# A residual block with linear attention: the DeltaNet keys turned to token order in 32x32 blocks by VectorE and the DRAM store

## The chip, the core and the metric

The kernel runs on one core of one Trainium2 chip. The core has TensorE (PE, matmuls and transposes against an identity), VectorE (DVE), ScalarE (ACT), GpSimd (POOL), and SyncE (SP), whose queue issues most of the DMAs; ACT and POOL issue some as well. The engines run their own instruction lists in order and wait for each other by semaphores. The metric is the device time of one execution in microseconds (us). Before the change it is 1882.36 us, the median of 3 runs (1882.15 to 1883.33).

## The reference

A hybrid residual block of width 1024 on 1024 tokens in float32: one wide projection feeds a gated linear attention branch (GLA, 4 heads) and a gated DeltaNet branch (GDN, 8 heads of 128); their gated sum is projected, and a squared-ReLU MLP follows. The change touches the GDN keys only:

```python
d_qkv = jax.nn.silu(causal_short_conv(d_qkv, gdn_conv_w))
d_q, d_k, d_v = jnp.split(d_qkv, [GDN_QK, 2 * GDN_QK], axis=-1)
d_k = l2_norm(d_k.reshape(bsz, s, GDN_HEADS, GDN_DK))
...
a_mat = jnp.where(strict, jnp.einsum('bhnid,bhnjd->bhnij', kb, k) * decay_mat, 0.0)
...
state = dc[..., None, None] * state + jnp.einsum('bhcd,bhcv->bhdv', ks, v_new)
```

Each key needs its l2 norm over the 128 channels of its head, for every token, and the state update needs the keys with tokens on the partitions.

## The kernel before

The wide projection is done as dense blocks: a block multiplies 128 columns of `w_in` (split in a high and a low part, `wH` and `wL`) with the normalised input (`hH`, `hL`) into one of two PSUM tiles `pm`, in 8 steps over the contraction. Each step is three rows of two 128x512 matmuls, in the order `hH,wH`, `hL,wH`, `hH,wL`, and one step is a tick of the program's clock. Everything else is hung on ticks: `at(dt, fn)` puts `fn` into an agenda, and it is emitted between two ticks. Until the second block of the branch gates every engine and SP keep the order in which the program emits; after that, the tile scheduler may reorder. The printed order of an engine's instructions is fixed when the kernel is built.

The first two key heads are made in the opening stage; six more dense blocks (`dense_n(6)`) give heads 2 to 7, then eight blocks give the branch gates (`branch_gate`). A finished key block is copied out by ACT (`key_copy`), gets three convolution taps and a SiLU on DVE (tile `cv`, channels on partitions, tokens along the free dimension), and then `key_head` works on it:

- `kT_d[h]` is stored as it is.
- `transposes(hf)`: four 128x128 TensorE transposes per half head into a PSUM tile of the `pa` pool (4 buffers).
- `squares(hf)`: ACT squares the four PSUM pieces with `accum_out`, which leaves the sums of squares per token in `ssK`, and copies the half into `ktok`; a store then writes `kt_d[h]`, tokens on rows. It is read again in the GDN heads, from 545 us on.
- `decays`, `grams`, `times`, `spill`: exponentials of the gate decays on ACT (tile `gr`), the products of keys with keys on TensorE, their product on DVE (`a`), and stores to `X_d`, `a21_d` and `Dt_d`.

`key_norms` adds EPS to `ssK`, takes the inverse root on DVE, transposes two results on TensorE (`nbrC`, `beC`) and stores them. From them `solve` starts: it loads `X_d`, runs 30 steps of elimination on DVE on two tiles (`X_1848` and `X_1849` in the order before, `X_1766` and `X_1767` after), and stores and reloads results; the ACT queue issues the stores `U_d`, `A_d` and `B_d`. Meanwhile the branch gates and then the first GLA head are computed. Their weights come by SP (`raw`), and ACT makes `wH` and DVE `wL`. `gla_gate(0)` lies in the same stretch: two products `lrS,wlrS`, then ACT, POOL and a scan on DVE (tiles `zm`, `b`).

`quad` is a constant 128x128 matrix with ones where row and column agree modulo 32; a matmul with it sums the four groups of 32 partitions.

Of the kernel before, what the change touches and what calls it, by code (L numbers as in the profile page):

```python
# [12 lines left out]
AF = mybir.ActivationFunctionType  # L13
ALU = mybir.AluOpType
# [36 lines left out]
def block_kernel(ctx: ExitStack, tc: tile.TileContext, x, c, ada_w, ada_b, pre_mix_w, post_mix_w,  # L51
# [25 lines left out]
    def t4(shape=(128, 1024), dt=F32, p="t", tag="w4"):  # L77
        return w4.tile(list(shape), dt, tag=tag, name=nm(p), bufs=tag_bufs[tag])
# [4 lines left out]
    def pat(shape=(128, 512)):  # L83
        return pa.tile(list(shape), F32, tag="pa", name=nm("pa"))
# [407 lines left out]
    def first_tiles():  # L492
        pk, pl = [pmt(), pmt()], [pat(), pat()]
        warm(pk[0][:, 0:128], 4)

        def wk_low(i):
            V.tensor_tensor(wk[i][1], raw_k[:, :, i * 128:(i + 1) * 128], wk[i][0].bitcast(F32), ALU.subtract)

        def mm(w, d, wlo, hlo, start, stop):

            for hf in range(2):
                hs_ = slice(hf * 512, (hf + 1) * 512)
                if w == 2:
                    last["pe"] = T.matmul(pl[hf][:64, :], wS[:, d, :], h_rhs(d, hf, hlo), start=start, stop=stop).ins
                else:
                    last["pe"] = T.matmul(pk[w][:, hs_], wk[w][wlo][:, d, :], h_rhs(d, hf, hlo), start=start, stop=stop).ins

        def a_(p, ws=(0, 2, 1)):
            for d in (2 * p, 2 * p + 1):
                for w in ws:  # L510
                    mm(w, d, 0, 0, d == 0, False)

        def b_(p, w):
            for d in (2 * p, 2 * p + 1):
                mm(w, d, 1, 0, False, False)

        def c_(p, w):
            for d in (2 * p, 2 * p + 1):
                mm(w, d, 0, 1, False, d == 7)

        wk_low(0)
        low(0)
        wk_low(1)
        a_(0, (0,))
        b_(0, 0)
        a_(0, (1,))

        fill = {1: ((c_, 0, 0), (b_, 0, 1), (c_, 0, 1)),
                2: ((a_, 0, (2,)), (a_, 1, (2,)), (b_, 1, 0), (c_, 1, 0)),
                3: ((c_, 0, 2), (c_, 1, 2), (b_, 2, 0), (b_, 1, 1), (c_, 1, 1))}  # L530
        for p in range(1, 4):
            f = [lambda e=e: e[0](*e[1:]) for e in fill[p]]
            ada_pe(p)
            ada_out(p)
            f[0]()
            ada_fin(p)
            ada_cols(p)
            high(p)
            if p == 1:
                A.copy(wS[:, :, 0:32], raw_lba)  # L540
            for fn in f[1:]:
                fn()
            low(p)
            if p == 1:
                V.tensor_tensor(wS[:, :, 32:64], raw_lba, wS[:, :, 0:32].bitcast(F32), ALU.subtract)
            if p == 2:
                ahead[1] = next(ahead[0])
            a_(p, (0, 1) if p == 1 else (0, 2, 1))
        b_(3, 0)
        c_(2, 0)  # L550
        c_(3, 0)
        y0 = key_copy(0, pk[0])
        c_(2, 2)
        c_(3, 2)
        sb, sb2 = t4((64, 1024), p="lba"), t4((64, 1024), p="lb2")
        for hf in range(2):
            A.copy(sb2[:, hf * 512:(hf + 1) * 512], pl[hf][0:64, :])
        for p in (2, 3):
            b_(p, 1)
        for p in (2, 3):  # L560
            c_(p, 1)
        for s_ in (1, 2, 3):
            key_tap(0, pk[0], y0, s_)
        t0 = key_tanh(y0)
        y1 = key_copy(1, pk[1])
        V.tensor_copy(sb[0:32], sb2[32:64])
        V.tensor_add(sb[0:32], sb[0:32], sb2[0:32])
        key_silu(y0, t0)
        for s_ in (1, 2, 3):
            key_tap(1, pk[1], y1, s_)  # L570
        return sb, y0, y1
# [177 lines left out]
    def key_head(h, k, on, tr, sq, ex, gram, times_):  # L749

        z = {}

        def transposes(hf):
            z[hf] = pt = pat()
            for i in range(4):
                T.transpose(pt[:, i * 128:(i + 1) * 128], k[:, (hf * 4 + i) * 128:(hf * 4 + i + 1) * 128], ident)

        def squares(hf):
            if not hf:
                z["tok"] = t4(p="ktok")  # L760
            pt = z.pop(hf)
            for i in range(4):
                j = hf * 4 + i
                A.activation(z["tok"][:, j * 128:(j + 1) * 128], pt[:, i * 128:(i + 1) * 128], AF.Square,
                             accum_out=ssK[:, h * 8 + j:h * 8 + j + 1])
            A.copy(z["tok"][:, hf * 512:(hf + 1) * 512], pt)

        def decays(hf):

            gr = Dk[h]  # L770
            for t in range(hf * 4, hf * 4 + 4):
                A.activation(gr[:, t * 128:(t + 1) * 128], gr[:, t * 128:(t + 1) * 128], AF.Exp,
                             bias=gcN[:, h * 8 + t:h * 8 + t + 1])

        def grams(hf):
            z["g", hf] = pt = pat()
            for i in range(4):
                kk = k[:, (hf * 4 + i) * 128:(hf * 4 + i + 1) * 128]
                T.matmul(pt[:, i * 128:(i + 1) * 128], kk, kk, start=True, stop=True)

        def times(hf):
            if not hf:
                z["a0"] = t4(p="a0")
            h_ = slice(hf * 512, (hf + 1) * 512)
            V.tensor_mul(z["a0"][:, h_], z.pop(("g", hf)), Dk[h][:, h_])

        def spill():
            Dk.pop(h)
            a3 = r3(z["a0"])
            xv = X_d[h * 16:(h + 1) * 16].rearrange("(t e) j i -> e j t i", e=2)  # L790
            DMA.dma_start(xv[0], a3[0:64, :, 0:64])
            DMA.dma_start(xv[1], a3[64:128, :, 64:128])
            DMA.dma_start(a21_d[h], a3[0:64, :, 64:128])

        on(tr[0], lambda: DMA.dma_start(kT_d[h], k))
        for hf in range(2):
            on(tr[hf], lambda hf=hf: transposes(hf))
            on(sq[hf], lambda hf=hf: squares(hf))
            on(ex[hf], lambda hf=hf: decays(hf))
            on(gram[hf], lambda hf=hf: grams(hf))  # L800
            on(times_[hf], lambda hf=hf: times(hf))
        on(sq[1] + 1, lambda: DMA.dma_start(kt_d[h], z["tok"]))
        on(ex[1] + 1, lambda: DMA.dma_start(Dt_d[h], Dk[h]))
        on(times_[1] + 1, spill)
        if h > 3:
            on(ex[0] - 8, lambda: load_decay(h))
            on(ex[0] - 3, lambda: mask_decay(h))
# [1 line left out]


    def key_norms():
        V.tensor_scalar(ssK, ssK, EPS, None, ALU.add)
        r = rsqrt(ssK, 64)
        V.tensor_mul(rbC, r, betaC)
        V.scalar_tensor_tensor(nbrC, rbC, -1.0, r, ALU.mult, ALU.mult)
        V.scalar_tensor_tensor(beC, beC, -1.0, r, ALU.mult, ALU.mult)

        n2 = nbrC.rearrange("p (t e) -> p e t", e=2)
        V.tensor_copy(nbrX[64:128], n2[64:128, 0])
        V.tensor_copy(nbrX[0:64], n2[64:128, 1])  # L820
        ps = pat()
        T.transpose(ps[0:64, 0:128], nbrC, ident)
        T.transpose(ps[0:64, 128:256], beC, ident)
        nb = t4((128, 256), p="nbr")
        V.tensor_copy(nb[0:64], ps[0:64, 0:256])
        ST.dma_start(be_d.rearrange("h (t q) -> (h t) q", q=128), nb[0:64, 0:128])
        ST.dma_start(ner_d.rearrange("h (t q) -> (h t) q", q=128), nb[0:64, 128:256])
# [623 lines left out]
    def masks():  # L1451
# [3 lines left out]
                        pattern=[[1, 128]], channel_multiplier=-1)  # L1455
        G.tensor_copy(cmask, causal)

    sb_lba, *keys = first_tiles()
    masks()
    raws0[C_DK + 512] = load_w(w_in, C_DK + 512)  # L1460
# [3 lines left out]
    def on(t, fn):  # L1464
        at(begin + t - clock[0], fn)
# [477 lines left out]
    def turn(hf, a, g):  # L1943

        pt = pat()
        for i in range(2):
            for e in range(2):
                T.transpose(pt[:, i * 256 + e * 128:i * 256 + e * 128 + 128],
                            xhs[4 * hf + a + e][:, (2 * g + i) * 128:(2 * g + i + 1) * 128], ident)
        if F[hf][g] is None:  # L1950
            F[hf][g] = pair_tile("F")
        for i in range(2):
            k = 2 * g + i
            o, src = F[hf][g][:, i, a * 128:(a + 2) * 128], pt[:, i * 256:(i + 1) * 256]
            if hf == 0 and (g % 2 if a else g > 1):
                V.tensor_scalar(o, src, am2[:, k:k + 1], sh2[:, k:k + 1], ALU.mult, ALU.add)
            else:
                A.activation(o, src, AF.Identity, scale=am2[:, k:k + 1], bias=sh2[:, k:k + 1])
# [579 lines left out]
```

## Time and profile before

| what | value |
|---|---|
| median of 3 runs | 1882.36 us |
| profiled execution: its time, its span | 1881.92 us, 1880.2 us |
| DVE, ACT, POOL busy share of the span | 74%, 47%, 8% |
| queue q1, share of 16 DMA engines | 45.4% |
| first and last `ktok` square on ACT | 75.6 us, 178.2 us |
| first load of `kt_d` in a GDN head | 545.6 us |

The profile describes one execution. A row of the timeline is: start in us, duration in us, engine, line, operation, output<-inputs, shape, and how many instructions were merged; in brackets the idle time of the engine just before and what ended it. All lines read L38, a helper, so groups are told apart by tiles. Matmuls are pipelined, so the duration of one is longer than the distance between the starts of two. A number after an underscore in the printed orders is a buffer, and buffer numbers differ between the two kernels.

### The profile page before, as it was taken

What the parts mean: (1) busy time and instruction counts of PE and PEld (TensorE: products, weight loads), DVE (VectorE), ACT (ScalarE), POOL (GpSimd) and SP (SyncE); (2) the same over time, 40 slices, a digit from 0 to 9 for tenths busy, and PEclk for the clock granted to TensorE, in tenths of its full rate; (3) what the DMA queues carried; (4) which work ended last, traced back from release to release, by engine and by line L of the source; (5) the groups of instructions that cost most, each with busy time, mean ns of one, the idle gap of its engine ahead of it and who ended that gap; (6) DMA issues with size and microseconds to landing.
All of it is one profiled execution on the core that took longest, in us unless ns stands there. A gap on an engine that the chain in (4) does not pass through costs nothing. (4 is left out here: it accounts for less than half of the span.)

```text
span 1880.2 us, 26321 instructions
## 1 busy us (share of the span) xinstructions
PE 1855.1 (99%) x10119; PEld 1556.2 (83%) x10119; DVE 1393.6 (74%) x2166; ACT 883.7 (47%) x1529; POOL 156.0 (8%) x148
## 2 busy tenths in 40 slices
PE   7999999999999999999999999999999999999998
PEld 5788888989898888888888888878888888888886
DVE  5664744968766677778788678986787877778887
ACT  5574324242333444444664555668644446443333
POOL 2120111010110000000101001000022210000001
PEclk9999999999999999999999999999999999999999
DMA  9695563223125454544868657256667668163425
GB/s 313 208 266 181 168 146 102 79 79 113 57 80 158 126 145 145 144 145 145 262 176 223 217 141 203 84 174 208 217 208 250 215 228 317 58 224 111 158 101 101
DMA packets 253341, 313.79 MB, mean 167 GB/s; under 512 B 72770, under 2 KB 178704, under 8 KB 253216
## 3 DMA queue, kind: packets, MB, share of 16 engines
q1 hardware_dynamic: 222608, 274.73, 45.4%
q0 software_dynamic: 14336, 22.44, 6.6%
q10 hardware_dynamic: 16272, 14.95, 2.5%
q8 instruction: 79, 1.29, 0.3%
q14 instruction: 46, 0.38, 0.1%
HBM read 231.67 MB, written 80.41 MB: 166 GB/s over the span
## 5 line engine op out<-in xcount | busy, mean ns | idle before, releaser
L38 PE MATMUL pm<-hH,wH 128*128 128x512 f32 x864 | 285.9, 412 | 0.0
L38 PE MATMUL pm<-hL,wH 128*128 128x512 f32 x864 | 269.0, 393 | 0.0
L38 PE MATMUL pm<-hH,wL 128*128 128x512 f32 x864 | 267.1, 390 | 0.0
L38 PE MATMUL pm<-oH,wB 128*128 128x512 f32 x672 | 214.5, 394 | 0.0
L38 PE MATMUL pa<-w,yH 128*128 128x512 f32 (+1 forms) x696 | 212.4, 387 | 0.0
L38 PEld LDWEIGHTS pm<-hH,wL 128*128 128x128 f32 x864 | 162.2, 188 | 36.8
L38 PEld LDWEIGHTS pm<-hL,wH 128*128 128x128 f32 x864 | 162.1, 188 | 35.9
L38 PEld LDWEIGHTS pm<-hH,wH 128*128 128x128 f32 x864 | 145.1, 190 | 17.0
L38 DVE TENSOR_TENSOR w<-raw,w 128x512 fp32r<-128x512 f32 (+1 forms) x144 | 125.6, 875 | 40.9 <-ACT w L38 37.4
L38 PEld LDWEIGHTS pa<-w,yH 128*128 128x128 f32 x696 | 130.1, 188 | 27.0 <-DVE ya L38 0.4
L38 PEld LDWEIGHTS pm<-oH,wB 128*128 128x128 f32 x672 | 126.2, 188 | 25.7 <-DMA wB<-in_w_branch_gla_dram 0.2
L38 ACT CAST w<-raw 128x512 fp32r<-128x512 f32 (+1 forms) x144 | 99.5, 711 | 89.0 <-DVE raw L38 79.8
L38 PE MATMUL pa<-w,yL 128*128 128x512 f32 (+1 forms) x348 | 134.5, 387 | 0.0
L38 PE MATMUL pm<-oL,wB 128*128 128x512 f32 x336 | 130.8, 389 | 0.0
L38 PE MATMUL pa<-oB,w 128*128 128x512 f32 x480 | 111.9, 391 | 0.8 <-DVE oB L38 0.5
L38 PEld LDWEIGHTS pa<-oB,w 128*128 128x128 f32 x480 | 89.6, 188 | 20.2 <-DVE oB L38 1.3
L38 ACT CAST wH<-raw 128x1024 fp32r<-128x1024 f32 x62 | 64.5, 1047 | 83.0 <-PE pm L38 51.1
L38 DVE SCALAR_TENSOR_TENSOR cv<-pm,ccol,cv 128x1023 f32<-128x1023 f32 (+2 forms) x72 | 92.0, 1278 | 14.1 <-ACT cv L38 12.9
L38 DVE TENSOR_TENSOR wL<-raw,wH 128x1024 fp32r<-128x1024 f32 x62 | 75.9, 1227 | 33.1 <-ACT wH L38 33.0
L38 PE MATMUL pm<-oT,w 128*128 128x512 f32 x384 | 90.8, 389 | 0.0
L38 PE MATMUL pa<-oT,w 128*128 128x512 f32 x384 | 90.8, 389 | 0.0
L38 DVE TENSOR_TENSOR ya<-pa,ya 128x512 f32<-128x512 f32 (+1 forms) x83 | 55.9, 682 | 43.7 <-PE pa L38 43.7
(423 smaller groups left out, 3725.8 us busy)
## 6 DMA issues: line engine op xcount, KB each, us to landing
yL<-y_d SPq DMA_DIRECT2D x53, 512.0 KB, 7.2
raw<-in_mlp_w_dram SPq DMA_DIRECT2D x23, 1024.0 KB, 6.1
raw<-in_w_in_dram SPq DMA_DIRECT2D x18, 1024.0 KB, 7.3
raw<-in_w_in_dram SPq DMA_DIRECT2D x32, 512.0 KB, 4.7
araw<-in_ada_w_dram SPq DMA_DIRECT2D x32, 512.0 KB, 3.8
raw<-in_mlp_w_dram SPq DMA_DIRECT2D x18, 512.0 KB, 5.3
araw<-in_ada_w_dram SPq DMA_DIRECT2D x32, 256.0 KB, 6.9
sl<-sg_d SPq DMA_DIRECT2D x16, 512.0 KB, 7.2
```

Of the source, the lines that this page charges most:

```text
L38: r = fn(*args, **kw)
```

## The change

The TensorE transposes go. DVE transposes each half of `cv` in 32x32 blocks into one tile (still called `ktok`); four DMAs per head, each from 32 partitions, put the blocks in their places in `kt_d[h]`. ACT squares the turned tile in one instruction into a new tile `kj`, and DVE sums groups of 32 into 32 columns of a new tile `ssr`, which lives through the whole stage. `key_norms` first multiplies `quad` with `ssr`, which adds the four channel groups, and four small DVE instructions put the sums in `ssK`.

```diff
-        def transposes(hf):
-            z[hf] = pt = pat()
-            for i in range(4):
-                T.transpose(pt[:, i * 128:(i + 1) * 128], k[:, (hf * 4 + i) * 128:(hf * 4 + i + 1) * 128], ident)
-
-        def squares(hf):
+        def turn(hf):
             if not hf:
-                z["tok"] = t4(p="ktok")
-            pt = z.pop(hf)
-            for i in range(4):
-                j = hf * 4 + i
-                A.activation(z["tok"][:, j * 128:(j + 1) * 128], pt[:, i * 128:(i + 1) * 128], AF.Square,
-                             accum_out=ssK[:, h * 8 + j:h * 8 + j + 1])
-            A.copy(z["tok"][:, hf * 512:(hf + 1) * 512], pt)
+                z["kb"] = t4(p="ktok")
+            h_ = slice(hf * 512, (hf + 1) * 512)
+            V.transpose(z["kb"][:, h_], k[:, h_])
+
+        def spread():
+
+            dst = kt_d[h].rearrange("(b i) (t c j) -> c i t b j", i=32, t=8, j=32)
+            for c_ in range(4):
+                DMA.dma_start(dst[c_], z["kb"][32 * c_:32 * c_ + 32].rearrange("i (t b j) -> i t b j", t=8, j=32))
+
+        def squares():
+            z["kj"] = t4(p="kj")
+            A.activation(z["kj"], z["kb"], AF.Square)
+
+        def sums(hf):
+            o = h * 32 + hf * 16
+            V.reduce_sum(ssr[0][:, o:o + 16], r3(z["kj"][:, hf * 512:(hf + 1) * 512], 16), axis=mybir.AxisListType.X)
...
-            on(tr[hf], lambda hf=hf: transposes(hf))
-            on(sq[hf], lambda hf=hf: squares(hf))
+            on(tr[hf], lambda hf=hf: turn(hf))
+            on(sq[1] + 1 + hf, lambda hf=hf: sums(hf))
...
-        on(sq[1] + 1, lambda: DMA.dma_start(kt_d[h], z["tok"]))
+        on(sq[1], squares)
+        on(tr[1] + 1, spread)
...
     def key_norms():
-        V.tensor_scalar(ssK, ssK, EPS, None, ALU.add)
+        ps = pat()
+        T.matmul(ps[:, 0:256], quad.rearrange("p a b -> p (a b)"), ssr[0], start=True, stop=True)
+        for c_ in range(4):
+            q = slice(32 * c_, 32 * c_ + 32)
+            V.tensor_scalar(ssK[q], ps[q, 0:256].rearrange("p (x c) -> p c x", c=4)[:, c_], EPS, None, ALU.add)
...
+    ssr = [t4((128, 256), p="ssr")]
```

On SP, around the store of head 6's keys, the rows before are:

```order
L38 DMA kT_d_446<-cv_1387 128x1024
L38 DMA Dt_d_462<-gr_1431 128x1024
L38 DMA kt_d_454<-ktok_1534 128x1024
L38 DMA X_d<-a_1589 64x8x64 x2
L38 DMA a_d_470<-a_1589 512x1x64
L38 DMA raw_1624<-in_w_in_dram 128x8x256
```

and now:

```order
L38 DMA kT_d_446<-cv_1333 128x1024
L38 DMA kt_d_454<-ktok_1457 256x4x32 x4
L38 DMA Dt_d_462<-gr_1368 128x1024
L38 DMA X_d<-a_1511 64x8x64 x2
L38 DMA a_d_470<-a_1511 512x1x64
L38 DMA raw_1548<-in_w_in_dram 128x8x256
```

One store of whole rows has become four, ahead of `Dt_d`; the load of the gates' weights (`raw`) is still the sixth name in the list.

On DVE, from the gates' small chain (`s`) of the first key block, the rows before are:

```order
L38 TENSOR_SCALAR s_776<-s_776,dtb 64x128
L38 SCALAR_TENSOR_TENSOR cv_760<-si_795,cv_760 128x1024
L38 TENSOR_SCALAR s_776<-s_776 64x128
L38 TENSOR_TENSOR wL_833<-raw_182,wH_787 128x1024
L38 TENSOR_SCALAR s_776<-s_776 64x128 x2
L38 TENSOR_TENSOR s_776<-s_776 64x128
L38 RECIPROCAL s_776<-s_776 64x128
L38 TENSOR_TENSOR s_776<-s_776 64x128 x2
L38 SCALAR_TENSOR_TENSOR s_776<-s_776 64x128
```

and now:

```order
L38 STREAM_TRANSPOSE ktok_799<-cv_726 128x512
L38 TENSOR_SCALAR s_777<-s_777,dtb 64x128
L38 SCALAR_TENSOR_TENSOR cv_761<-si_796,cv_761 128x1024
L38 TENSOR_SCALAR s_777<-s_777 64x128
L38 STREAM_TRANSPOSE ktok_799<-cv_726 128x512
L38 TENSOR_TENSOR wL_821<-raw_182,wH_788 128x1024
L38 TENSOR_SCALAR s_777<-s_777 64x128 x2
L38 TENSOR_TENSOR s_777<-s_777 64x128
L38 RECIPROCAL s_777<-s_777 64x128
L38 TENSOR_TENSOR s_777<-s_777 64x128
L38 TENSOR_REDUCE ssr_504<-kj_832 128x16
L38 STREAM_TRANSPOSE ktok_851<-cv_761 128x512
```

A second reduction follows these, and then the rest of the chain; three transposes and two reductions now stand ahead of its end.

Also on DVE, inside the elimination, the first rows of the GLA gate (`zm` from `pa`) stand before between these:

```order
L38 TENSOR_TENSOR X_1848<-X_1848,Xt_1920 128x22x9
L38 TENSOR_TENSOR X_1849<-X_1849,Xt_1920 128x22x9
L38 TENSOR_SCALAR zm_2038<-pa_2054,vcol 128x512
L38 TENSOR_SCALAR zm_2038<-pa_2068,vcol 128x512
L38 TENSOR_TENSOR Xt_1920<-X_1848 128x184
```

and now:

```order
L38 TENSOR_TENSOR X_1767<-X_1767,Xt_1838 128x15x16
L38 TENSOR_TENSOR X_1766<-X_1766,Xt_1838 128x19x12
L38 TENSOR_SCALAR zm_1956<-pa_1972,vcol 128x512
L38 TENSOR_SCALAR zm_1956<-pa_1986,vcol 128x512
L38 TENSOR_TENSOR Xt_1838<-X_1767 128x240
L38 TENSOR_TENSOR wL_2064<-raw_2061,wH_2063 128x1024
```

The first number of a shape is the step: the gate's rows stood after step 22 of both tiles and now stand after step 19 of one and step 15 of the other.

## The prediction

> **What bounds the kernel now.** I read the page's summary first, then whom TensorE waited for, then the table of stretches, then the timeline of the key stage.
>
> ```profile
> span 1880.2 us, 26321 instructions
> PE 1855.1 (99%) x10119; PEld 1556.2 (83%) x10119; DVE 1393.6 (74%) x2166; ACT 883.7 (47%) x1529; POOL 156.0 (8%) x148
> ...
> PE pm L38 <- DVE x L38: 9.9, 1, 9.9
> PE pa L38 <- ACT rs L38: 0.9, 2, 0.5
> ...
> 140.00:160.00 20.00, 20.00 (x108) 17.07 (x107) 14.07 (x15) 12.71 (x41) 1.09 (x1) 1.00 0.38 131
> ```
>
> TensorE (PE) is busy 99% of the span. Its waits say more than that share: the longest is 9.9 us, once, in the opening, and the next pair is 0.9 us in total. From 140 to 160 us, inside the key stage, PE is busy all 20 us at a granted clock of 1.00, DVE 14.07 us and ACT 12.71. So PE's queue sets the end, and a row taken out of it shortens the span by what it added between the starts of its neighbours, as long as no other engine then comes too late.
>
> **What PE loses: 7.0 us.**
>
> ```profile
> 93.66 0.60 PE L38 MATMUL pa<-ident,cv 128*128 128x128 f32 x4
> 94.01 0.71 PE L38 MATMUL pm<-hH,wH 128*128 128x512 f32 x2
> ...
> 95.48 0.62 PE L38 MATMUL pm<-hH,wH 128*128 128x512 f32 x2
> ...
> 96.86 0.62 PE L38 MATMUL pm<-hH,wH 128*128 128x512 f32 x2
> ...
> L38 ACT ACTIVATE ktok<-pa x64: 253/272/295, 75.6 to 178.2; 128x128 f32<-128x128 f32 x64
> L38 PE MATMUL pa<-ident,cv 128*128 128x128 f32 x128 | 27.1, 273 | 0.0
> ```
>
> From 93.66 to 95.48 PE starts one group of four transposes and one step (three rows) of the dense block: 1.82 us. From 95.48 to 96.86 it starts one step alone: 1.38 us. A group costs 0.44 us. ACT squared 64 pieces, so there are 64 transposes in 16 groups: 16 x 0.44 = 7.0 us.
>
> The durations must not be summed: 64 x 273 ns would be 17.5 us, but they overlap their neighbours. The Trainium skill, "TensorE: Matmul & The Clock Gate", section "Part 4: PE-mode transpose", says that a 128x128 transpose took about 275 ns inside one kernel. The row's 273 ns agrees as a duration; taken as the price, it would give an estimate of 17.6 us here, which the starts contradict.
>
> **What PE gets: 0.5 us.** One float32 product of `quad` with 256 columns of `ssr`.
>
> ```profile
> 102.31 1.05 PE L38 MATMUL pa<-cv 128*128 128x128 f32 x8
> 103.11 0.71 PE L38 MATMUL pm<-hH,wH 128*128 128x512 f32 x2
> ```
>
> Four key products of 128 columns (each recorded as two) take 0.80 us from start to start, 0.20 each. The trace has no product of this shape; by columns it is 0.4 us, at most the 0.8 of the four, at least the 0.2 of one. With the slower first pair behind such a switch I take 0.5.
>
> **What DVE and ACT get, and where it is hidden.**
>
> ```profile
> L38 DVE STREAM_TRANSPOSE sqt<-qj x16: 701/702/706, 608.3 to 939.2; 128x512 f32<-128x512 f32 x16
> L38 DVE TENSOR_REDUCE sqr<-sqt x16: 685/686/689, 609.1 to 939.9; 128x16 f32<-128x512 f32 x16
> L38 ACT ACTIVATE qj<-cv x8: 1047/1048/1061, 587.2 to 911.0; 128x1024 f32<-128x1024 f32 x8
> ```
>
> The GDN queries already use these three forms. Per head DVE gets 2 x 0.70 + 2 x 0.69 = 2.8 us, 22 us in all. Nearly two heads' worth fits into the 20 us stretch above: 14.07 + about 4 is still under 20, so the load is hidden by PE's dense blocks; without that cover it would cost the 22 us. ACT exchanges eight squares with accumulators and two copies for one square of 1.05 us and gets lighter. What can cost is not load but lateness at places where PE waits next. I found four.
>
> *First, the gates' chain at 86 us: 0.5 us.*
>
> ```profile
> 75.58 0.28 DVE L38 TENSOR_SCALAR s<-s,dtb 64x128 f32<-64x128 f32 x1 [1.20 <-DMA s<-ba_d]
> 81.27 0.28 DVE L38 TENSOR_TENSOR s<-s 64x128 f32<-64x128 f32 x1 [1.00 <-ACT s L38]
> 82.75 0.28 DVE L38 TENSOR_SCALAR s<-s 64x128 f32<-64x128 f32 x1
> 86.13 0.31 ACT L38 ACTIVATE s<-s 64x128 f32<-64x128 f32 x1
> 86.34 0.43 PE L38 MATMUL pa<-ident,s 64*128 64x64 f32 x3
> ```
>
> The chain `s` ends on DVE at 82.75 + 0.28 = 83.03, an exponential on ACT at 86.13 follows, and PE transposes the results at 86.34, the third of them with that exponential. Now three transposes and two reductions, 3.5 us, stand ahead of the chain's end. The idle 1.20 us before 75.58 takes the first one; the second and the rest outrun the idle 1.00 us before 81.27, so the chain ends about 1.4 us later, at 84.45, and the exponential at 84.8 (ACT, without its squares, is free by then). Four groups gone bring PE there at 86.34 - 1.8 = 84.5. I take a wait of 0.5 us for the third transpose, between 0 and 1.2. Behind it on PE's queue is everything.
>
> *Second, the gate weights at 178 us, and the chain to `ssr`: no wait, by a few tenths.*
>
> ```profile
> 164.96 0.63 SPq L38 DMA_DIRECT2D raw<-in_w_in_dram  x1
> 172.53 1.05 ACT L38 CAST wH<-raw 128x1024 fp32r<-128x1024 f32 x1 [7.06 <-DMA raw<-in_w_in_dram]
> 173.61 1.23 DVE L38 TENSOR_TENSOR wL<-raw,wH 128x1024 fp32r<-128x1024 f32 x1 [11.16 <-ACT wH L38]
> 177.91 0.62 PE L38 MATMUL pm<-hH,wH 128*128 128x512 f32 x2
> ```
>
> Before, the weights were ready at 174.84 and first needed two rows after 177.91, a spare of 3.5 us. Now PE starts that block 6.5 us earlier, at 171.4 (16 groups less the wait above). The load stands on SP behind `X_d`, which waits for DVE's last product of head 6; that has 14 groups less ahead of it, minus about 0.9 us for the transpose before the taps and the reduction before it. So `raw` is issued 4.8 us earlier, at 160.15, and the spare shrinks by 1.7 to 1.8 us. Behind `wL` on DVE stand both transposes of head 7 (1.35), then ACT's square (1.1), a reduction, the product, a reduction (2.1): `ssr` is whole 4.5 us after `wL`, at 174.4. PE reaches its product eight rows of 0.455 into the block, at 175.0. No wait, by about 0.5 us.
>
> *Third, the inverse root.*
>
> ```profile
> 178.63 0.20 DVE L38 TENSOR_SCALAR ssK<-ssK 128x64 f32<-128x64 f32 x1 [0.32 <-ACT ktok L38]
> 182.53 0.22 DVE L38 SCALAR_TENSOR_TENSOR nbrC<-rbC,rs 128x64 f32<-128x64 f32 x1
> ```
>
> From `ssK` to `nbrC` DVE took 4.1 us with a `wL` of 1.2 in between, which is now ahead of it; with three more small rows it is 3.3 us after the product's end at 175.5, or 3.9 us if that `wL` is late. PE gets to transpose `nbrC` nine rows after the product, at 179.6. No wait.
>
> *Fourth, the elimination.* It is in DVE's order that this differs most.
>
> ```profile
> 223.80 0.69 ACT L38 ACTIVATE b<-pa,vcol 128x512 f32<-128x512 f32 x1 [0.40 <-PE pa L38]
> 227.87 1.40 DVE L38 TENSOR_SCALAR zm<-pa,vcol 128x512 f32<-128x512 f32 x2
> 235.09 2.29 DVE L38 TENSOR_TENSOR_SCAN b<-smask,zm 128x1024 f32<-128x1024 f32 x1 [2.29 <-POOL zm L38]
> 257.01 2.00 ACT L38 CAST wH<-raw 128x1024 fp32r<-128x1024 f32 x2 [5.84 <-DVE zm L38]
> 267.14 0.28 PE L38 MATMUL pm<-wH,hH 128*128 128x256 f32 x1
> ```
>
> Before, DVE came to `zm` at 227.87, when its inputs from PE and ACT (223.80) were long there. Now the two rows stand some steps earlier, and DVE must wait there for PE and ACT, and again for POOL before the scan, with the rest of the elimination queued behind. So the elimination gains little of PE's lead: I let it end at the same time as before. The ACT queue issues its stores, and the cast at 257.01 stands behind them. PE needed that weight's first product at 267.14; the second half, `wL`, was done 2.3 us after the cast began, so the spare was 7.8 us. PE comes 6.0 us earlier: 1.8 us are left. No wait, but this is the softest point.
>
> **The stores.** Each of the four DMAs per head moves 128 KB in runs of 32 floats, 128 bytes.
>
> ```profile
> kt_d<-ktok SPq DMA_DIRECT2D x8, 512.0 KB, 4.2
> ...
> 260.02 2.43 SPq L38 DMA_DIRECT2D Xs<-A_d  x4
> ...
> 300.31 6.41 SPq L38 DMA_DIRECT2D U_d<-Xs  x4
> ...
> 242.00:244.00 2.00, 2.00 (x11) 1.65 (x10) 0.35 (x4) 0.00 (x0) 1.70 (x2) 1.00 1.10 385
> 248.00:250.00 2.00, 2.00 (x10) 1.66 (x9) 0.00 (x0) 1.84 (x2) 0.00 (x0) 1.00 1.38 216
> ```
>
> The kernel has such DMAs: four loads with these runs took SP 2.43 us to issue, four stores 6.41 us (behind a full queue), against 0.32 us for the one store of rows. While the stores `U_d<-X`, also in such runs, were under way the DMAs moved 216 GB/s (248 to 250 us), against 385 in the stretch from 242; so 512 KB take about 2.4 us instead of 1.4. Nobody reads `kt_d` before 545 us, so its own landing (4.2 us before) costs nothing. I take 2.6 us of issue, which ends before `X_d` is due. The Trainium skill, "DMA: Bandwidth & Descriptors", section "Specifications", says that transfers under 512 bytes miss line rate, because the DMA engine then reads, modifies and writes; it speaks against this store. The trace agrees in direction, 216 against 385 GB/s, and the rule by itself gives no other sum; what it does here is the first rival.
>
> **The sum.** -7.0 + 0.5 + 0.5 = -6.0 us. Against the profiled execution, 1881.92 us with 1.7 us around its span, that gives 1875.9; the median of the runs is 0.44 higher, so the prediction is **1876.4 us**.
>
> **Rivals.** *The stores back up SP's queue.* If four of them take the 6.41 us of `U_d<-Xs`, `X_d` and the gate weights go out 2.8 us later, past the spare of 1.8: a wait of 1.0 for `wL`, then about 1.3 more for `ssr`, which stands on the same chain; 1876.4 + 2.3 = 1878.7. For it: 216 GB/s. Against it: the DMA share from 140 to 160 us is 0.38, so no full queue.
>
> *The elimination comes late.* If DVE's two waits push it 4 us beyond what I reckon, PE waits 4 - 1.8 = 2.2 us, and the time is 1878.6. The same mechanism gives the slower side: each further us costs one, so past 7.8 us of lateness the kernel is slower than before; with 12 us it would be 1886.6. For it: two waits on DVE's own queue where there was one. Against it: a whole `zm` chain took only 11 us before.
>
> *The change gains nothing:* the lead is given back at several of these places, 1881 to 1883. Against it: each has been spare before.
>
> *Transposes priced by duration:* 17.5 us less, 1866. The starts exclude it nearly.
>
> **How the numbers follow.** My forecast, 1875 to 1878, has 0.62; the stores 0.13; the late elimination within 4 us 0.10; nothing gained 0.08; slower 0.05; still faster 0.02. The range takes the lower end from no wait at all and the 0.2 product (1875.6), less 1 us for small waits elsewhere that may fall away, and reaches over the first two rivals with about 2 us for both together: 1874.6 to 1880.5. About 0.2%, 3.8 us, is what a measurement of this kernel tells from no change; that line is at 1878.6, in the middle of the first two rivals, so half of their 0.23 and the forecast make faster 0.76, same 0.18, slower 0.06.
>
> **What would show it.** Right: PE's rows in the key stage 0.455 us apart without gaps at the old places; one wait of about half a us at the three `s` transposes; the `quad` product's neighbours 0.5 us apart; the block that began at 177.91 beginning near 171.4. Wrong: a PE wait for `wL` or for `ssr` near 172 to 175 us (the stores or DVE), a wait for `wH` near 261 us (the elimination), or four stores that hold SP over 3 us a head.

## The result, and the profile after

| | before | after |
|---|---|---|
| median | 1882.53 us (1882.0 to 1883.67, 6 runs) | 1894.64 us (1891.85 to 2701.58, 6 runs) |
| ratio | | 1.006, 95% interval [1.0046, 1.0073] |
| profiled execution, its span | 1881.92 us, 1880.2 us | 1891.85 us, 1890.1 us |

The kernel became 0.6% slower, some 12 us, where 6 us less were forecast. One run of 2701.58 us, at a granted clock of 0.645, is left out of the ratio; without it the median after is 1894.13 us, and as no trace was taken of it, nothing below explains it.

The page of the kernel after, its head:

```profile
span 1890.1 us, 26139 instructions
## 1 busy us (share of the span) xinstructions
PE 1850.0 (98%) x10057; PEld 1552.2 (82%) x10057; DVE 1415.7 (75%) x2201; ACT 866.3 (46%) x1393; POOL 152.9 (8%) x148
```

PE is busy 5.1 us less than before (1855.1) and the span is 9.9 us longer, so PE must stand still somewhere. The waits of PE in the kernel after (who waits, for whom, then us in total, times, the longest):

```profile
PE pm L38 <- ACT wH L38: 14.6, 1, 14.6
PE pm L38 <- DVE x L38: 9.9, 1, 9.9
PE pa L38 <- ACT sts L38: 0.8, 1, 0.8
```

The second row was there before. The first is new: one wait, 14.6 us, for a weight. The timeline of the kernel after shows where, with the rows of SP and ACT that lead to it:

```profile
142.09 0.93 SPq L38 DMA_DIRECT2D kt_d<-ktok  x1
...
160.01 0.34 ACTq L1396 DMA_DIRECT2D sg_d<-sig  x1
...
162.66 1.31 SPq L38 DMA_DIRECT2D kt_d<-ktok  x2
...
165.84 1.05 PE L38 MATMUL pa<-cv 128*128 128x128 f32 x8
...
169.01 0.61 PE L38 MATMUL pm<-hH,wL 128*128 128x512 f32 x2
...
176.43 0.64 SPq L38 DMA_DIRECT2D raw<-in_w_in_dram  x1
...
183.09 1.04 ACT L38 CAST wH<-raw 128x1024 fp32r<-128x1024 f32 x1 [23.11 <-DMA raw<-in_w_in_dram]
184.19 1.22 PE L38 MATMUL pm<-hH,wH 128*128 128x512 f32 x2 [14.56 <-ACT wH L38]
185.21 1.06 PE L38 MATMUL pm<-hL,wH 128*128 128x512 f32 x2
...
188.45 0.62 PE L38 MATMUL pm<-hH,wL 128*128 128x512 f32 x2
188.91 0.62 PE L38 MATMUL pm<-hH,wH 128*128 128x512 f32 x2
```

Read it backwards. PE stands from 169.6 to 184.2 us for the weights of the third gate block, the second of the four places that the prediction named. Their load was issued at 176.43 us; in the kernel before it was issued at 164.96. SP was late by then because it had issued the first store `kt_d` of head 5 at 142.09 us and the second only at 162.66. Between them it did nothing for 19.6 us, and the queue's own waits say for what:

```profile
SPq L38 <- DMA sg_d<-sig: 20.4, 2, 19.6
```

`sg_d<-sig` is a store of the branch gates. ACT issues it, at 160.01 us. It shares no data with `kt_d`. What joins the two is in the built program. A completion semaphore is a counter that a DMA raises when it is done. The DMAs of SP and ACT use eight of them, printed as DMAHW0 to DMAHW7, in turn, and a DMA first waits for the one before it on its semaphore. The printed order of the kernel after, with waits and row numbers, SP first and then the one row of ACT:

```
93 L38 DMA kt_d4_452<-ktok302_1239 256x4x32 [waits DMAHW4_49,DVE_49]
94 L38 DMA kt_d4_452<-ktok302_1239 256x4x32 [waits DMAHW5_49]
95 L38 DMA kt_d4_452<-ktok302_1239 256x4x32 [waits DMAHW6_49]
96 L38 DMA kt_d4_452<-ktok302_1239 256x4x32 [waits DMAHW0_49]
...
102 L38 DMA kt_d5_453<-ktok337_1347 256x4x32 [waits DMAHW6_49,DVE_49]
103 L38 DMA kt_d5_453<-ktok337_1347 256x4x32 [waits DMAHW7_49]

103 L1396 DMA sg_d0_0_493<-sig421_1546 128x1024 [waits DMAHW7_49,Activation_49]
```

Between the third and the fourth store of head 4 the turn jumps from 6 to 0. The 7 went to the gate store on ACT, which runs some 25 us after those stores of SP, and the next to get 7 is the second store of head 5. Before the change the first gate store had semaphore 0 between two DMAs of head 6, and the next on 0 was the second store `X_d` of head 7, which came much later anyway.

One more loss shows in the table of stretches of the kernel after. Columns: the stretch, its length, busy time (and rows) of PE, PE's weight loads, DVE, ACT and POOL, the granted clock, DMA share, GB/s.

```profile
170.00:174.00 4.00, 0.00 (x0) 0.00 (x0) 0.00 (x0) 0.00 (x0) 0.00 (x0) 1.00 0.98 229
174.00:176.00 2.00, 0.00 (x0) 0.00 (x0) 0.00 (x0) 0.00 (x0) 0.00 (x0) 0.65 1.00 317
176.00:184.00 8.00, 0.00 (x0) 0.00 (x0) 0.00 (x0) 0.91 (x1) 0.00 (x0) 0.50 0.90 247
184.00:188.00 4.00, 3.81 (x9) 3.07 (x10) 3.29 (x5) 3.84 (x11) 0.00 (x0) 0.50 0.01 2
188.00:190.00 2.00, 2.00 (x9) 1.60 (x9) 2.00 (x4) 1.54 (x2) 0.00 (x0) 0.94 1.01 194
```

The granted clock falls to 0.50 while PE stands and stays there when it starts again: five rows of two matmuls take 188.45 - 184.19 = 4.26 us instead of 5 x 0.455 = 2.28, where 0.455 us is the distance between such rows at the full clock. That is 2.0 us on top of the wait. The Trainium skill, "TensorE: Matmul & The Clock Gate", section "Part 1: The HAM clock gate (the "warmup" mystery)", says that the clock halves after an idle window of about 3.4 us and comes back after about as much of steady work. The trace agrees in kind: the clock is full until 174 us, 4.4 us after PE's last row, and full again 4.3 us after the restart.

So the sum of this execution: at its last key products PE was 174.26 - 165.84 = 8.4 us ahead of the kernel before (0.8 of it from the opening, where the first dense row starts at 66.89 us against 67.69; e1 below, with 67.83, has none of it). It then lost 14.6 + 2.0 us, 0.55 for the `quad` product, and about 1.1 in gaps at 272 to 302 us that are taken up below. That is 18.2 us lost against 8.4 gained, 9.8 us in all, where the spans differ by 9.9.

### The profile page after: what moved, and what is told of

Read it like the earlier page. It is cut to its first block, busy times and chain, and to the rows that moved or that the text cites. A ratio compares the mean times of both kernels' runs of the same rounds, so it can differ in the third digit from the quotient of the medians.

```text
span 1890.1 us, 26139 instructions
## 1 busy us (share of the span) xinstructions
PE 1850.0 (98%) x10057; PEld 1552.2 (82%) x10057; DVE 1415.7 (75%) x2201; ACT 866.3 (46%) x1393; POOL 152.9 (8%) x148
## 5 line engine op out<-in xcount | busy, mean ns | idle before, releaser
L38 PE MATMUL pm<-hH,wH 128*128 128x512 f32 x864 | 285.9, 412 | 14.6 <-ACT wH L38 14.6
```

The lines of the kernel that those rows point to most:

```text
L38: r = fn(*args, **kw)
```

## The experiments

Theory A is the shared semaphore. Theory B is the prediction's first rival, that four stores in runs of 128 bytes fill SP's queue. Theory C is the other order of the elimination on DVE. All ratios are against the kernel before on the same chip, with 95% intervals. In e2, e3 and e7 the blocks of the turned keys are not put in their places, so `kt_d` holds other data there; these three serve for their times alone.

| run | median, us | ratio to before | PE wait for `wH` |
|---|---|---|---|
| e1: changed kernel, gate store's semaphore moved | 1879.47 | 0.9984 [0.9975, 0.9994] | none |
| e2: four stores of whole rows | 1885.41 | 1.0015 [1.0005, 1.0024] | 6.1 |
| e3: one store of whole rows | 1877.48 | 0.9974 [0.9962, 0.9985] | none |
| e4: kernel before, four stores of short runs | 1883.83 | 1.0007 [0.9998, 1.0017] | none |
| e5: e1 with the product four rows later | 1877.92 | 0.9976 [0.9967, 0.9984] | none |
| e6: kernel before, gate store's semaphore moved | 1891.11 | 1.0045 [1.0032, 1.0059] | 7.1 |
| e7: e2 with the gate store's semaphore moved | 1876.89 | 0.9972 [0.9961, 0.9982] | none |
| e8: changed kernel, stores issued by POOL | 1878.73 | 0.9980 [0.9971, 0.9989] | 1.2 |

**e1, only the semaphore.** The edge below only says that a gate store (all eight of them have it) gets its turn after the last DMA that SP had been given by then; it adds no wait.

```diff
-            at(4, lambda s_=s_, j=j: ST.dma_start(sig_d[0][j // 2][j % 2], s_))
+            at(4, lambda s_=s_, j=j: gate_store(s_, j))
...
+    def gate_store(s_, j):
+        st = ST.dma_start(sig_d[0][j // 2][j % 2], s_)
+        tc.add_manual_dep(st.ins, DMA.recent.name,
+                          mybir.DependencyInfo(mybir.DependencyClass.NoSync, mybir.DependencyReason.DATA),
+                          reason="lane order")
```

> Same instructions in the same order on every engine as the changed kernel; only the semaphores that the DMAs get differ: the first gate store sg_d<-sig now shares its semaphore with the second store X_d of head 7 on SP, instead of with the second store kt_d of head 5. Theory A (shared semaphore: SP stood 19.6 us before that kt_d store because the gate store before it on the same semaphore was issued by ACT only at 160.0 us): SP's gap at 143 to 162 us goes, the PE wait of 14.6 us for wH near 170 us goes, the granted clock stays at 1.00 there; the 14.6 us and about 2 us of half clock come back: 1876 to 1879 us. Theory B (the 128-byte runs fill SP's queue, as in the first rival of the prediction): the same stores, so the wait stays, 1891 to 1895 us. Theory C (the other order of the elimination on DVE costs the time): the order is the same, so a PE wait for wH near 261 us shows and the time is over 1882 us.

Measured: 1879.47 us, 14.7 us below the 1894.13 us of the changed kernel, with the same instructions. Their order is not quite the same on every engine: on ACT the second gate store now comes behind two small stores, `be_d` and `ner_d`, after 181 us and so after the place of the loss. The timeline of e1 around the stores of head 5, the gate store and the load (PEld is PE's weight load):

```profile
143.84 4.46 SPq L38 DMA_DIRECT2D kt_d<-ktok  x4
...
160.91 0.34 ACTq L1400 DMA_DIRECT2D sg_d<-sig  x1
161.23 0.64 SPq L38 DMA_DIRECT2D raw<-in_w_in_dram  x1
...
166.74 1.05 PE L38 MATMUL pa<-cv 128*128 128x128 f32 x8
169.34 1.05 ACT L38 CAST wH<-raw 128x1024 fp32r<-128x1024 f32 x1 [8.46 <-DMA raw<-in_w_in_dram]
...
171.70 0.30 PEld L38 LDWEIGHTS pm<-hH,wL 128*128 128x128 f32 x2 [0.50 <-DVE wL L38]
...
174.13 0.61 PE L38 MATMUL pm<-hL,wH 128*128 128x512 f32 x2
175.92 0.70 PE L38 MATMUL pa<-ssr,quad 128*128 128x256 f32 x2 [1.18 <-DVE ssr L38]
176.27 0.82 PE L38 MATMUL pm<-hH,wL 128*128 128x512 f32 x2
176.93 0.62 PE L38 MATMUL pm<-hH,wH 128*128 128x512 f32 x2
...
255.18 2.00 ACT L38 CAST wH<-raw 128x1024 fp32r<-128x1024 f32 x2 [7.93 <-issue]
258.06 1.22 DVE L38 TENSOR_TENSOR wL<-raw,wH 128x1024 fp32r<-128x1024 f32 x1
260.88 0.28 PE L38 MATMUL pm<-wH,hH 128*128 128x256 f32 x1
```

The 20 us gap is gone; the four stores take 4.46 us in one go. B and C fall as the cause of the loss: the stores and DVE's order are as in the changed kernel. A stands, though the time is 0.5 us above its range. Against the prediction 3 us are still missing; among them are a wait of 1.18 us for `ssr` and a few tenths where PE's weight load waits for `wL`.

**e2 and e3, whole rows.** In both the turned tile is stored as it lies, in rows of 4 KB.

```diff
-            dst = kt_d[h].rearrange("(b i) (t c j) -> c i t b j", i=32, t=8, j=32)
-            for c_ in range(4):
-                DMA.dma_start(dst[c_], z["kb"][32 * c_:32 * c_ + 32].rearrange("i (t b j) -> i t b j", t=8, j=32))
+            for c_ in range(4):
+                DMA.dma_start(kt_d[h][32 * c_:32 * c_ + 32], z["kb"][32 * c_:32 * c_ + 32])
```

In e3 the loop is one `DMA.dma_start(kt_d[h], z["kb"])`.

> Four stores per head as in the changed kernel, but of whole rows of 4 KB (the blocks are not put in place, so kt_d holds other data). Here the gate store shares its semaphore with the store a_d of head 5, still before the load of the gate weights. Theory A: SP stands from about 141 to 162 us all the same; after that about ten DMAs of 0.4 to 1.3 us stand ahead of the load, so it is issued near 168 us and PE waits 5 to 8 us; 1881 to 1886 us. Theory B: without the short runs nothing is late, 1876 to 1878 us, no PE wait over 1 us near 170 us.

> One store of whole rows per head instead of four (the blocks are not put in place, so kt_d holds other data); the gate store shares its semaphore with X_d of head 7, as before the change. Theories A and B both: no wait near 170 us, 1876 to 1878 us, which is what the change without its stores is worth (-7.0 for the transposes, +0.5 for the product, +0.5 for the s transposes). Theory C: a wait near 261 us if the order of the elimination is still the changed one.

Measured: 1885.41 and 1877.48 us. SP's timeline in e2:

```profile
144.68 1.27 SPq L38 DMA_DIRECT2D X_d<-a  x2
161.45 0.52 SPq L38 DMA_DIRECT2D a_d<-a  x1
...
168.65 0.78 SPq L38 DMA_DIRECT2D raw<-in_w_in_dram  x1
```

SP stands 15.5 us before the store `a_d` of head 5, the one that shares the gate store's semaphore here, and PE waits 6.1 us; the time of the load, the wait and the run's time are as A had them. No run is short in e2, so B cannot explain it. With one store per head (e3) the gate store shares its semaphore with a store `X_d` of head 7, as before the change, and there is no wait for `wH`.

**e4, the stores alone in the kernel before.**

```diff
-        on(sq[1] + 1, lambda: DMA.dma_start(kt_d[h], z["tok"]))
+        def spread():
+            dst = kt_d[h].rearrange("p (t c j) -> p t c j", c=4, j=32)
+            src = z["tok"].rearrange("p (t c j) -> p t c j", c=4, j=32)
+            for c_ in range(4):
+                DMA.dma_start(dst[:, :, c_], src[:, :, c_])
+        on(sq[1] + 1, spread)
```

> The kernel before, with TensorE's transposes and ACT's squares, and only its one store per head replaced by four that move the same tile in runs of 128 bytes. The gate store shares its semaphore with the third store kt_d of head 7, which comes after it anyway. Theory A: four issues of about 0.7 us instead of one of 0.32 on SP, 2.5 us a head, inside a spare of 3.5 us: 1882 to 1884 us, no new PE wait over 1 us. Theory B: the short runs fill the queue as they do in the changed kernel, and PE waits near 178 us: 1892 to 1899 us.

Measured: 1883.83 us, 1.5 us over before with an interval that holds 1: no change that this can tell, where B asked for 10 us or more. PE does not wait for `wH`, but it has a new wait behind it, a little over the 1 us that A allowed:

```profile
PE pa L38 <- DVE nbrC L38: 1.2, 1, 1.2
```

So the four short stores cost something, but not the loss that was to be explained.

**e6, the semaphore alone in the kernel before.** The same edge the other way round: the store `kt_d` of head 4 takes its turn after the first gate store.

```diff
...
+        if not j:
+            tc.add_manual_dep(kt_ins[4], st.ins.name,
+                              mybir.DependencyInfo(mybir.DependencyClass.NoSync, mybir.DependencyReason.DATA),
+                              reason="semaphore order")
```

> The kernel before, with the same instructions; in the key stage every engine and SP keep their order. Only the turn of the first gate store sg_d on the shared semaphores is put earlier, ahead of the store kt_d of head 4, so that the second store X_d of head 5 on SP shares its semaphore and must wait for it. Theory A: SP stands from about 149 us until the gate store, issued at 165.5 us, has landed near 168 us; nine DMAs later, near 174 us, the load of the gate weights is issued, their cast ends near 182 us, and PE, which needs them at 178, waits 4 to 6 us: 1886 to 1889 us, though nothing of the change is in it. Theory B: without the short runs and the four stores nothing happens, 1882 to 1883 us.

Measured: 1891.11 us, 8.9 us slower than before, with nothing of the change in it. SP's wait for the gate store, and the timeline of e6:

```profile
SPq L38 <- DMA sg_d<-sig: 19.9, 1, 19.9
```

```profile
147.47 0.32 SPq L38 DMA_DIRECT2D kt_d<-ktok  x1
...
164.80 0.35 ACTq L1392 DMA_DIRECT2D sg_d<-sig  x1
167.80 1.26 SPq L38 DMA_DIRECT2D X_d<-a  x2
...
175.57 0.63 SPq L38 DMA_DIRECT2D raw<-in_w_in_dram  x1
...
184.47 1.22 PE L38 MATMUL pm<-hH,wH 128*128 128x512 f32 x2 [7.11 <-ACT wH L38]
185.50 1.05 PE L38 MATMUL pm<-hL,wH 128*128 128x512 f32 x2
...
189.76 0.77 PE L38 MATMUL pm<-hH,wH 128*128 128x512 f32 x2
```

The table of stretches of e6, columns as above:

```profile
180.00:190.00 10.00, 5.53 (x13) 4.37 (x14) 3.07 (x6) 6.56 (x28) 0.00 (x0) 0.50 0.34 124
```

The mechanism is shown from the other side. In the elimination DVE's order came out otherwise here too, but no wait of PE is new except this one. The time is 2 us over the expected range: the load came 1.6 us later than reckoned, the wait is 7.1 us where 4 to 6 were expected, and the half clock, which the expectation left out, makes six rows take 5.29 us instead of 2.73.

**e7, both cures.** e2 with the edge of e1.

> As e2 (four stores of whole rows, so kt_d holds other data) with the gate store's semaphore moved as in e1. Theory A: the gap of SP at 145 to 161 us and the 6.1 us wait for wH go. If the length of the runs costs what separates e1 (1879.5) from e3 (1877.5), it comes to 1877.5 us as e3; if the number of stores does, to 1879.5 us as e1. Theory B: no change against e2, 1885.4 us.

Measured: 1876.89 us; the 6.1 us wait is gone. Against e1 (1879.47) only the length of the runs differs, against e3 (1877.48) only the number of stores. So the runs of 128 bytes seem to cost some 2 us in all, 0.6 of them in the wait for `ssr`, and four stores instead of one nothing; the intervals of e1 and e7 still overlap a little.

**e5, the product later.** In e1's kernel the call of `key_norms` moves from tick 17 to 20; the product then stands four rows of PE later.

```diff
-    at(17, key_norms)
+    at(20, key_norms)
```

> As e1 (the gate store's semaphore moved), and the product of quad with ssr stands four rows of PE later, so that PE does not reach it before DVE's last reduction. In e1 PE stood 1.18 us for ssr. Theory A2 (what is left of the prediction in e1 is the chain to ssr behind a later load of the gate weights): that wait goes, a wait of up to 0.5 us for nbrC, eight rows behind, comes instead: 0.7 to 1.2 us less than e1, 1878.3 to 1878.8 us. Rival (the rest lies elsewhere, PE only waits at another place): 1879.5 us as e1.

Measured: 1877.92 us, 1.5 us below e1; the wait for `ssr` is gone, and only 0.15 us for `nbrC` came. The gain is a little over its range, and the intervals of the two overlap. Among the kernels that put the keys in their places this has the lowest median, 0.24% below the kernel before, though e8 cannot be told from it.

**e8, the stores on POOL**, whose DMAs have semaphores of their own.

```diff
-                DMA.dma_start(dst[c_], z["kb"][32 * c_:32 * c_ + 32].rearrange("i (t b j) -> i t b j", t=8, j=32))
+                G.dma_start(dst[c_], z["kb"][32 * c_:32 * c_ + 32].rearrange("i (t b j) -> i t b j", t=8, j=32))
```

> The changed kernel with the four stores of runs of 128 bytes issued by POOL instead of SP; POOL's DMAs have semaphores of their own, SP has one store fewer than before. The product of quad stands four rows later here. Theory A: nothing on SP waits for a gate store, raw is issued near 159 us as in e3, no PE wait over 0.7 us: 1876.5 to 1878.5 us. Rival (POOL issues these stores slowly, and the loads of gr, which stand behind them on POOL, come late; with them a, X_d and the gate weights): a PE wait for wH or gr, 1880 us or more.

Measured: 1878.73 us, 0.2 us over A's range and below the rival's 1880. The gap of SP is gone here too, but the load was issued at 162.21 us, not near 159, and PE waits 1.2 us for `wH`. POOL's timeline and SP's in e8:

```profile
154.73 3.96 POOL L38 DMA_DIRECT2D kt_d<-ktok  x4 [5.81 <-DVE ktok L38]
...
159.90 2.27 SPq L38 DMA_DIRECT2D a_d<-a  x1
162.21 2.00 SPq L38 DMA_DIRECT2D raw<-in_w_in_dram  x1
```

POOL needs about 1.0 us for each store, SP 0.69 (median in e1). About half of SP's delay against e3 is the issue of `a_d`, just ahead of the load, which took 2.27 us instead of 0.64. This is the only POOL run, so the cause stays open.

## Why the prediction was wrong

**The step that failed** is the second place: "`raw` is issued 4.8 us earlier, at 160.15", and with it "No wait". It was issued at 176.43. The step followed DVE's queue, on which the stores ahead of the load wait, and took the four new DMAs as issue time only. It did not ask what each of them itself waits for. With the 24 more DMAs of SP the turns on the eight semaphores fell otherwise, and one store came to stand behind a gate store of ACT. e1 (the wait goes when only the turn moves) and e6 (it comes without the change) show it. The number of DMAs does not decide it: e4 has the same 24 more, and its gate store shares with a store of head 7. What in the build gave the gate store this early turn was not tried.

**The first rival** named the place and the sign, a wait for these weights, but not the mechanism nor the size: 2.3 us against 16.6. Short runs are neither needed for the loss (e2) nor enough (e4). On a small scale what it describes is there: in e1 the stores of heads 4 and 5 hold SP for 4.7 and 4.5 us, over the 3 us that the prediction gave as a sign against itself, and the price is about the 2 us between e1 and e7. The rule of the Trainium skill on transfers under 512 bytes ("DMA: Bandwidth & Descriptors", section "Specifications"), that they miss line rate, bears on no more than these.

**The transposes, -7.0.** Right, a little small. From the first to the last key products of this stage, with 11 groups between, the kernel before takes 174.26 - 99.59 = 74.67 us, e1 166.74 - 97.41 = 69.33. PE's timelines of before and then of e1, whose last row (166.74) stands above:

```profile
99.59 1.05 PE L38 MATMUL pa<-cv 128*128 128x128 f32 x8
...
174.26 1.05 PE L38 MATMUL pa<-cv 128*128 128x128 f32 x8
```

```profile
97.41 1.05 PE L38 MATMUL pa<-cv 128*128 128x128 f32 x8
```

That is 0.485 us a group, not 0.44; 16 groups are 7.8.

**The product, +0.5.** Right: in e1 it starts at 175.92 and the second row behind it at 176.93; less one row, 1.01 - 0.455 = 0.55.

**The `s` transposes, +0.5.** A wait is there, of half the size. The third transpose in the kernel after:

```profile
83.91 0.27 PE L38 MATMUL pa<-ident,s 64*128 64x64 f32 x1 [0.26 <-ACT s L38]
```

**`ssr`, "no wait, by about 0.5 us".** Wrong by a small size: 1.18 us in e1. PE began the block at 170.44, about a us earlier than reckoned, mostly since the groups are worth more, and the load went out at 161.23 instead of 160.15, behind stores that hold SP 3 to 5 us a head, not 2.6. In e7, whose stores of whole rows hold it 1.7 to 1.8 us a head there, the load goes out at 158.85 and the wait is 0.6 us. So the spare of 1.8 us for `wL` was gone as well: PE's weight load waits 0.50 us for it in e1, although the spare before, by the prediction's own rows, was nearer 4.0 us than 3.5 (two rows after 177.91 is 178.82, and the weights were ready at 174.84). In e5 the wait for `ssr` is gone.

**The inverse root** was right to within 0.2 us (the 0.15 of e5), and **the elimination** was right. In e1 the last `wL` is done at 258.06 + 1.22 = 259.28 and PE needs its first product at 260.88: 1.6 us of spare where 1.8 were forecast.

**Not foreseen:** small gaps later. `kt` is first loaded at 542.2 us in e1, 3.4 us earlier than before, and the span ends 2.1 us earlier. PE, 4.8 us ahead of the kernel before from 190 us on, loses 1.5 us of that lead at 272 to 302 us; two of the gaps stand there as waits for nothing that the profile shows, in rows of small matmuls. The timeline of PE in e1:

```profile
274.13 0.28 PE L38 MATMUL pm<-wH,hL 128*128 128x256 f32 x1 [0.52 <-issue]
...
295.12 0.25 PE L38 MATMUL pa<-Xs,Xs 32*32 32x32 f32 x5 [0.48 <-issue]
```

Their cause was not tried, nor was that of the last us or so of the lead, which goes between 900 and 1250 us.

## What to carry to other kernels

When a change adds or removes DMAs, print the waits of the built program and look up, for each DMA, which one had its completion semaphore before it and on which queue that one is issued: a wait for a DMA of another engine that runs later is a trap, and here a single ordering edge took it away. The order of each engine's instructions does not show it; only the waits do. Where PE sets the end and stands for long, add the half clock after it to the price: here it came after waits of 6.1 (e2), 7.1 and 14.6 us, and not after one of 1.2 us (e8).

## What was not expected of the hardware

- After 14.6 us of standing still PE ran at a granted clock of 0.50 for 4.3 us, after 7.1 us (e6) for 5.3 us: 2.0 and 2.6 us on top of the waits, so the longer wait did not cost more.
- While SP stood at that wait the DMA engines stood too. The stretch from 150 to 160 us of the kernel after, columns as above:

```profile
150.00:160.00 10.00, 10.00 (x54) 8.57 (x53) 7.69 (x9) 4.32 (x7) 1.09 (x1) 1.00 0.02 7
```

In the kernel before, the same stretch has a share of 0.36 and 105 GB/s. A DMA share of 0.02 beside a gap of 19.6 us in SP is what told here that the queue waited and was not full.
